# TensorE instead of SyncE as the engine that ends a log-sum-exp kernel

## The chip, the cores and the metric

The kernel runs on 1 core of one Trainium2 chip. The metric is the device time in microseconds (us). The core has five engines, each with its own instruction stream: TensorE (PE), VectorE (DVE), ScalarE (ACT), GpSimd (POOL) and SyncE (SP). An engine named with a q behind it (SPq, PEq) is that engine's sequencer, which handles waits, semaphores, branches and DMA issues itself.

## What is computed

The reference takes x of 32 x 512 x 1024 float32 and returns, for each of the 16,384 rows of 1024, the logarithm of the sum of exponentials:

```python
max_x = np.max(x, axis=-1, keepdims=True)
return (max_x.squeeze(-1) + np.log(np.sum(np.exp(x - max_x), axis=-1))).astype(np.float32)
```

## The kernel before, in words

Each of the 128 partitions holds 128 rows of 1024. The kernel does not subtract the maximum at first: it takes exp of the raw data and sums it, and a check at the end tells whether all sums are in a safe range. Only if one is not does it do the work again with the maximum taken off (the block under `nc.If`, line 258), which the inputs here do not need.

SP issues 18 loads of falling size, written out in the table `LOADS` (lines 17 to 22), into a ring of 48 rows per partition (`load`, lines 121 to 128). For each load ACT waits on a semaphore of its own (`landed`), takes exp in place (line 192), and DVE sums the rows (line 196, or line 204 for the last rows of the stream). Every engine's order is written by hand, and every wait is on a counter: `act`, `dve` and `pe` count finished instructions, and a DMA adds 16 to its semaphore when it has landed.

The end goes like this. ACT takes the logarithm of the first 112 rows (line 219), and SP stores them early (line 227, semaphore `early_store`, called `sp.sem`). PE adds up the last sums with small matmuls (lines 143, 147 and 248), so that DVE can tell with one comparison whether all is fine (`fine`, line 251). Meanwhile ACT takes the last logarithms (lines 230 and 232), and SP issues the last store (line 236, semaphore `stored`). ACT and DVE read `fine` into a register each (line 254) and branch past the second pass. Then both add 1 to `done` (lines 303 and 304).

The lines after that are those of the change. In the kernel before they all run on SP: it waits for `done` to reach 2 and for the early store (lines 305 and 306), clears all semaphores but `stored` with one instruction (line 307), and with a last instruction waits for `stored` to reach 16 and takes the 16 off again (line 309). It is the program's last instruction. POOL does nothing but set constants at the program's start. PE's last instruction is the matmul of line 147 that adds the last partial sum.

At the program's start the language puts barriers between the five engines (lines 57 and 347 in the profile): each engine adds to one semaphore with a DRAIN, POOL counts them and adds to a second one, and each engine waits for that one with an EVENT_SEMAPHORE.

Of the kernel before, what the change touches and what calls it, by code (L numbers as in the profile page):

```python
# [47 lines left out]
def kernel(  # L48
# [5 lines left out]
    nc = tc.nc  # L54
# [49 lines left out]
    landed = [nc.alloc_semaphore(f"landed{i}") for i in range(len(loads))]  # L104
# [3 lines left out]
    sp = Counted(nc, nc.sync, "early_store")  # L108
    done = nc.alloc_semaphore("done")
    again = nc.alloc_semaphore("again")  # L110
    ready = nc.alloc_semaphore("ready")
    stored = nc.alloc_semaphore("stored")
# [145 lines left out]
    with nc.If(all_fine < 1):  # L258
# [43 lines left out]

    nc.scalar.sem_inc(done, 1)
    nc.vector.sem_inc(done, 1)
    nc.sync.wait_ge(done, 2)
    nc.sync.wait_ge(sp.sem, 16)
    nc.sync.sem_clear(range(landed[0].num, stored.num))
    kind = dict(sync_type="semaphore", id=stored.num, ant_name="stored")
    nc.sync.add_instruction(mybir.InstEventSemaphore(
        name=nc.get_next_instruction_name(), engine=mybir.EngineType.SP,  # L310
        sync_info=mybir.SyncInfo(
            on_wait=[mybir.SyncWait(wait_mode="sem-ge-imm", wait_value=16, **kind)],
            on_update=[mybir.SyncUpdate(update_mode="sem-sub-imm", update_value=16, **kind)],
# [49 lines left out]
```

## Time and profile before

| | us |
|---|---|
| median of 3 runs | 162.51 (162.45 to 162.53) |
| the profiled execution, its own time | 162.54 |
| its span, first to last instruction | 161.2 |
| time outside that span | 1.34 |
| DVE busy | 120.4 |
| ACT busy | 116.2 |
| PE busy | 2.1 |

All times in the profile are counted from the first instruction, which is SP's first load. The span is that of the program's own instructions. What the time of an execution holds beyond the span, 1.34 us, has no instruction in the profile, but the trace also records updates of semaphores, and some of these come after the program's last instruction.

### The profile page before, as it was taken

Reading aid. Unit: us, or ns where it says so; the run is one execution under the profiler, and the core shown is the slowest. Engines: PE = TensorE matmul, PEld = TensorE weight load, DVE = VectorE, ACT = ScalarE, POOL = GpSimd, SP = SyncE. Lnnn points to the kernel's source line nnn. Section 1 sums busy time; section 2 is a strip of 40 time slices with the busy share of each in tenths; the row PEclk is TensorE's granted clock in tenths of the full one; section 3 lists DMA queues with packets and bytes.
Section 4 is the critical chain, followed back from the end, with each engine's and each line's share of the span. In section 5 each row is a group of like instructions: output and inputs, shape, how many; then the busy total and the mean of one; then the engine's idle time right before and its main releaser. Section 6 shows DMA issues by size and latency. Waiting matters only on the chain.

```text
span 161.2 us, 227 instructions
## 1 busy us (share of the span) xinstructions
PE 2.1 (1%) x24; PEld 1.0 (1%) x24; DVE 120.4 (75%) x57; ACT 116.2 (72%) x49; POOL 0.2 (0%) x4
## 2 busy tenths in 40 slices
PE   0000000000000000000000000000000000000022
PEld 0000000000000000000000000000000000000011
DVE  0000000009999999999999999999999995999894
ACT  3000059990799709995199949983999999989995
POOL 0000000000000000000000000000000000000000
DMA  7996996996996996996999999997999999999991
GB/s 260 520 520 276 504 520 276 504 520 276 504 520 276 504 520 276 504 520 276 463 439 439 439 423 407 445 534 331 439 439 419 434 407 430 442 419 410 410 397 25
DMA packets 2883, 67.19 MB, mean 417 GB/s; under 512 B 577, under 2 KB 705, under 8 KB 1345
## 3 DMA queue, kind: packets, MB, share of 16 engines
q1 hardware_dynamic: 2880, 67.18, 97.3%
q14 instruction: 3, 0.02, 0.0%
HBM read 67.11 MB, written 0.07 MB: 417 GB/s over the span
## 4 chain that ended last, share of the span: by engine, by line
DVE 51%; DMA 29%; ACT 16%; issue 2%; PE 0%
DVE sumexp L196 51%; DMA ring<-in_x_dram 29%; ACT ring L192 15%; ACT last_exp L170 1%; ACT res L219 0%; PE count L147 0%; DVE fine L251 0%
## 5 line engine op out<-in xcount | busy, mean ns | idle before, releaser
L196 DVE TENSOR_REDUCE sumexp<-ring 128x8 f32<-128x8192 f32 (+6 forms) x15 | 108.8, 7326 | 36.3 <-ACT ring L192 36.3
L192 ACT ACTIVATE ring<-ring 128x8192 f32<-128x8192 f32 (+15 forms) x23 | 103.8, 4571 | 41.8 <-DMA ring<-in_x_dram 41.8
L204 DVE SCALAR_TENSOR_TENSOR ring<-ring 128x512 f32<-128x512 f32 x17 | 10.7, 689 | 0.6 <-ACT ring L192 0.6
L181 ACT ACTIVATE ring<-ring 128x1024 f32<-128x1024 f32 x9 | 9.4, 1041 | 0.0
L114 ACT ACT_TABLE_LOAD x1 | 1.3, 1283 | 1.5 <-PEq L57 1.5
L143 PE MATMUL count<-far,bad 128*1 128x1 f32 x2 | 0.2, 164 | 153.7 <-DVE clamped L138 153.7
L147 PE MATMUL count<-sumexp,ones 128*1 128x1 f32 x20 | 1.8, 164 | 3.5 <-DVE ring L204 3.4
L181 ACT ACTIVATION_READ_ACCUMULATOR ring<-ring 128x1 f32 x9 | 1.7, 186 | 0.0
L204 DVE DVE_READ_ACCUMULATOR ring<-ring 128x1 f32 x17 | 1.4, 83 | 0.0
L115 DVE MEMSET ones<- 128x1 f32 x1 | 0.1, 59 | 1.5 <-PEq L57 1.5
L170 ACT ACTIVATE last_exp<-ring 128x640 f32<-128x640 f32 (+1 forms) x2 | 1.2, 591 | 0.0
L143 PEld LDWEIGHTS count<-far,bad 128*1 128x1 f32 x2 | 0.1, 80 | 153.7 <-DVE clamped L138 153.7
L147 PEld LDWEIGHTS count<-sumexp,ones 128*1 128x1 f32 x20 | 0.8, 81 | 4.4 <-DVE ring L204 4.2
L251 DVE TENSOR_SCALAR fine<-count 1x1 int32<-1x1 f32 x1 | 0.1, 147 | 0.6 <-PE count L147 0.6
L170 ACT ACTIVATION_READ_ACCUMULATOR last_exp<-ring 128x1 f32 x2 | 0.4, 186 | 0.0
L138 DVE SCALAR_TENSOR_TENSOR clamped<-clamped,sumexp 128x119 f32<-128x119 f32 x1 | 0.3, 284 | 0.0
L232 ACT ACTIVATE res<-sumexp 128x1 f32<-128x1 f32 x1 | 0.3, 294 | 0.0
L219 ACT ACTIVATE res<-sumexp 128x112 f32<-128x112 f32 x1 | 0.3, 279 | 0.0
L242 DVE SCALAR_TENSOR_TENSOR clamped<-sumexp 128x9 f32<-128x9 f32 x1 | 0.2, 169 | 0.1
L133 DVE TENSOR_SCALAR clamped<-sumexp 128x119 f32<-128x119 f32 x1 | 0.2, 222 | 0.0
L230 ACT ACTIVATE res<-sumexp 128x15 f32<-128x15 f32 x1 | 0.2, 198 | 0.0
L248 PE MATMUL count<-far,bad 128*1 128x1 f32 x2 | 0.2, 164 | 0.0
(8 smaller groups left out, 0.7 us busy)
## 6 DMA issues: line engine op xcount, KB each, us to landing
ring<-in_x_dram SPq DMA_DIRECT2D x1, 6912.0 KB, 26.0
ring<-in_x_dram SPq DMA_DIRECT2D x1, 6400.0 KB, 23.9
ring<-in_x_dram SPq DMA_DIRECT2D x1, 4608.0 KB, 17.7
ring<-in_x_dram SPq DMA_DIRECT2D x1, 3840.0 KB, 19.3
ring<-in_x_dram SPq DMA_DIRECT2D x1, 2816.0 KB, 25.6
ring<-in_x_dram SPq DMA_DIRECT2D x1, 2368.0 KB, 25.2
ring<-in_x_dram SPq DMA_DIRECT2D x1, 1696.0 KB, 21.7
ring<-in_x_dram SPq DMA_DIRECT2D x1, 1248.0 KB, 24.4
```

The lines of the kernel that those rows point to most:

```text
L114: nc.scalar.preload_act_table_set("natural_log_exp_and_others")
L133: dve.did(nc.vector.tensor_scalar(out=clamped[:, 0:LATE], in0=sumexp[:, 0:LATE], scalar1=LOW, scalar2=HIGH, op0=ALU.max, op1=ALU.min,))
L138: dve.did(nc.vector.scalar_tensor_tensor(out=clamped[:, 0:LATE], in0=clamped[:, 0:LATE], scalar=0.0, in1=sumexp[:, 0:LATE], op0=ALU.bypass ...
L143: pe.did(nc.tensor.matmul(count, lhsT=bad[:, 0:1], rhs=far, start=True, stop=False))
L147: return pe.did(nc.tensor.matmul(count, lhsT=ones, rhs=sumexp[:, c : c + 1], **kw))
L170: at = act.did(nc.scalar.activation(out=last_exp[:, here - p : end - p], in_=ring[:, here:end], func=AF.Exp, accum_out=sumexp[:, LAST : NC ...
L181: at = act.did(nc.scalar.activation(out=v, in_=v, func=AF.Exp, accum_out=sumexp[:, c : c + 1]))
L192: at = act.did(nc.scalar.activation(out=v, in_=v, func=AF.Exp))
L196: who = (dve, dve.did(nc.vector.reduce_sum(out=sumexp[:, c : c + s], in_=rows, axis=AX.X)))
L204: who = (dve, dve.did(nc.vector.scalar_tensor_tensor(out=lo, in0=lo, scalar=1.0, in1=rows[:, r, H:d], op0=ALU.mult, op1=ALU.add, accum_out ...
L219: ln_early = act.did(nc.scalar.activation(out=res[:, 0:W], in_=sumexp[:, 0:W], func=AF.Ln))
L232: ln_last = act.did(nc.scalar.activation(out=res[:, LAST:NC], in_=sumexp[:, NC : NC + 1], func=AF.Ln, bias=sumexp[:, LAST:NC]))
```

## The change

The last instructions are moved from SP to PE. SP adds 1 to `done` after it has issued the last store, as ACT and DVE do, and PE waits for 3 instead of SP for 2. The clear and the last wait are the same instructions on another engine. Nothing else differs.

```diff
     nc.scalar.sem_inc(done, 1)
     nc.vector.sem_inc(done, 1)
-    nc.sync.wait_ge(done, 2)
-    nc.sync.wait_ge(sp.sem, 16)
-    nc.sync.sem_clear(range(landed[0].num, stored.num))
+    nc.sync.sem_inc(done, 1)
+    nc.tensor.wait_ge(done, 3)
+    nc.tensor.wait_ge(sp.sem, 16)
+    nc.tensor.sem_clear(range(landed[0].num, stored.num))
     kind = dict(sync_type="semaphore", id=stored.num, ant_name="stored")
-    nc.sync.add_instruction(mybir.InstEventSemaphore(
-        name=nc.get_next_instruction_name(), engine=mybir.EngineType.SP,
+    nc.tensor.add_instruction(mybir.InstEventSemaphore(
+        name=nc.get_next_instruction_name(), engine=mybir.EngineType.PE,
         sync_info=mybir.SyncInfo(
             on_wait=[mybir.SyncWait(wait_mode="sem-ge-imm", wait_value=16, **kind)],
             on_update=[mybir.SyncUpdate(update_mode="sem-sub-imm", update_value=16, **kind)],
```

## The prediction

> **What bounds the kernel now.** I read the chain of work that ended last first, then SP's own waits, then the last instructions one by one.
>
> ```profile
> ## 4 chain that ended last, share of the span: by engine, by line
> DVE 51%; DMA 29%; ACT 16%; issue 2%; PE 0%
> ```
>
> This says that the 161.2 us go to loads, ACT and DVE. The change touches none of those instructions: by the order of instructions on each engine, DVE, ACT and POOL keep theirs, SP loses the clear and the last wait, and PE gains them behind its last matmul. So only the last two microseconds can differ. The view of DMA issues has the last store (out<-in, size, us to landing):
>
> ```profile
> out_dram<-res SPq DMA_DIRECT2D x1, 8.0 KB, 1.7
> ```
>
> It lands 1.7 us after SP issues it; it is issued at 159.45, so it lands at 161.2, which is the end of the span. The chain of work ends before it, with the comparison at line 251, because it follows no store. The end is set by the store.
>
> ```profile
> SPq L307 <- ACTq L303: 0.7, 1, 0.7
> SPq L309 <- SPq L309: 0.6, 1, 0.6
> ```
>
> These are SP's own waits. SP stood 0.7 us before the clear, until ACT's addition to `done` at line 303, and then 0.6 us before its last instruction. The second is the wait for the store. The view of single lines gives both instructions:
>
> ```profile
> L307 SPq EVENT_SEMAPHORE_RANGE_CLEAR  x1: 68/68/68, 160.5 to 160.5; - x1
> L309 SPq EVENT_SEMAPHORE  x1: 17/17/17, 161.2 to 161.2; - x1
> ```
>
> From the trace's records at full precision: ACT's addition ends at 160.493, the clear runs from 160.516 to 160.584, the store's 16 increments of `stored` come from 160.731 to 161.175 (the 15th at 160.873), and the last instruction runs from 161.191 to 161.208.
>
> **What comes behind the span.** The trace also holds updates of a semaphore that the program does not use, number 2, after and between the engines' ends:
>
> ```
> 159.522 | 160.637  160.676  160.720 | 161.352  161.396  161.434  161.468  161.515
> then resets of the semaphores 7 to 255, 161.477 to 162.085
> 162.309  162.343  162.381  162.425  162.448  162.546  162.584  162.618  162.665
> ```
>
> Nine updates, twice. I read it as a barrier of five engines, a chain up and back (five updates up, four down). The first comes at 159.522. POOL was done by 1.6, DVE and ACT only after 160.3, SP at 161.208; only PE ends just before it (its last matmul at 159.343). So PE is the first link. The second comes at 160.637, 0.144 after ACT's end. The third and fourth are POOL and DVE, idle already. The fifth comes at 161.352, 0.144 after SP's end: the same 0.144 as ACT's, so SP is the last link. Now SP comes last and the way back starts at once: 161.515 - 161.352 = 0.163 us. The second barrier starts at PE and finds all others ready: 162.665 - 162.309 = 0.356 us. That is what the first would take if PE came last.
>
> [...]
>
> **The change, part by part.**
>
> *Removed from SP, added to SP.* SP's clear (68 ns) and last wait go; SP gets one addition to `done`. Its wait of line 306 ran at 159.849, and I take the addition there: 0.63 before ACT's, so `done` is still completed by ACT at 160.493. Nothing is queued behind SP's two instructions but its link in the barrier. Cost 0.
>
> *The clear on PE.* PE has been idle since 159.343, so no program work is queued behind its new wait. The trace does not show a clear on PE. From below, SP's 68 ns; from above, three times that, 0.2 us, as the widest ratio of PE to SP for a semaphore instruction (51 to 17 ns, next view). Started by 160.55 it ends by 160.75, and the store lands at 161.175. The store's landing hides it, at either end, with 0.4 to spare; without that cover it would cost 0.07 to 0.2. Cost 0.
>
> *The last wait on PE.* The barriers at the program's start show the same kind of instruction on all engines:
>
> ```profile
> L57 SPq EVENT_SEMAPHORE  x2: 17/17/17, 1.0 to 1.4; - x2
> L57 ACTq EVENT_SEMAPHORE  x2: 17/17/17, 1.1 to 1.4; - x2
> L57 DVEq EVENT_SEMAPHORE  x2: 21/21/21, 1.1 to 1.4; - x2
> L57 PEldq EVENT_SEMAPHORE  x2: 51/51/51, 1.1 to 1.4; - x2
> ```
>
> SP needs 17 ns, PE 51. The starts, at full precision, are 1.375 for SP and 1.387 for PE after the same release: PE wakes 0.012 later. From such a wait to the engine's next instruction, in two barriers, SP needs 71 and 92 ns, ACT 92 and 91, DVE 111 and 112, PE 150 and 151. So PE's sequencer is 1.64 (151/92) to 2.11 (150/71) times as slow as SP's here, on average 1.85.
>
> *From the last wait to PE's link.* SP needs 161.352 - 161.191 = 0.161 from the start of its last instruction to its update; ACT the same. For PE the trace shows no such stretch: behind its last matmul it needs 0.179 from the matmul's end and 0.342 from its start (159.180 to 159.522). By the ratios it is 0.161 x 1.64 = 0.264 to 0.161 x 2.11 = 0.340; I take 0.161 x 1.85 = 0.298, between PE's two rows. A gain is excluded: no row has PE quicker than SP.
>
> Sum: 0.012 (later waking) + 0.298 - 0.161 = 0.137 (slower instructions) + 0.193 (the barrier goes up behind PE) = 0.342 us. With the ends of the ratio it is 0.308 and 0.384. The 0.193 contains 0.054 because DVE, having just made its own update, answers SP after 0.098 and not 0.044; without it the lower end is 0.254. What follows the first barrier (resets, second barrier) starts at PE in both kernels and moves as a whole.
>
> Against the profiled execution this is 162.54 + 0.34 = 162.88. That one lies 0.03 above the median of the runs, so the forecast is 162.51 + 0.34 = **162.85 us**; its own range is 162.76 to 162.90.
>
> **The rivals.**
>
> *PE fetches its last code late* (slower). The records show two reads of 8192 bytes of instructions near the end, at 159.830 (0.342 long) and 161.078 (0.621 long). The first starts 0.308 after PE's link. If it is PE's code for the resets, it now has time; behind a late PE it would land 0.65 to 0.93 after PE's link, while the resets (first record at 161.736, 0.221 after the barrier) would want it 0.356 + 0.221 = 0.577 after. That adds 0.07 to 0.35: 162.92 to 163.20. For it: the place in time. Against it: SP and ACT also have work there, and the records do not name the engine.
>
> *PE's sequencer is as quick as SP's here.* Then 0.137 falls away and 0.012 + 0.193 = 0.205 is left: 162.72, within the bound. For it: the 0.179 behind the matmul's end is near SP's 0.161. Against it: 51 to 17 ns. [...]
>
> *The time ends before the barrier.* The 1.34 us outside the span can lie behind it (barrier, resets and second barrier end 1.46 after it) or ahead of it. If the time closes at the last engine's own end, only 0.012 + 0.034 counts: 162.56.
>
> *Faster: the time closes on an engine other than PE.* The decisive point is again where the 1.34 lies. If the time is closed by the end of an engine's program, and PE's is not the one read, the store's landing drops out of it: the last end would be ACT's, at 160.493 instead of SP's at 161.208, 0.715 earlier: 161.80. For it: PE's share of the end is the one that the span has never had to show. Against it: all five engines are in the barrier.
>
> That the change doesn't do what it says can be left out: PE's stream has the two instructions, and nothing else is behind the store.
>
> **How the numbers follow.** About 0.2% (0.33 us) can be told from no change. Forecast 0.52, of which I give 0.34 to above 162.84 and 0.18 to below, as the point lies just above the bound; late code 0.18, slower; PE as quick as SP 0.12, same; time before the barrier 0.10, same; closed on another engine 0.08, faster. So faster 0.08, same 0.40, slower 0.52. The range leaves out the faster case and the upper part of the late code (about 0.1): 162.55 to 163.00.
>
> **What would show it.** In the changed kernel's trace the store should land as before, at 161.18; PE's last EVENT_SEMAPHORE should start at 161.20 and take 51 ns; semaphore 2 should show its first update only some 0.3 after that, all nine in one run of about 0.356, and the second run as before. The span should grow by only 0.05, and the time outside it by 0.3. If the first update comes within 0.18 of PE's last instruction, PE is as quick as SP; if the resets of 7 to 53 start later than 0.22 after the ninth update, code is late. If the store lands earlier or later by more than 0.05, the change reaches something that I hold untouched, and the forecast is wrong in its ground.

## The result, and the profile after

The changed kernel takes 162.69 us (median of 15 runs, 162.58 to 163.12) against 162.50 for the kernel before in the same comparison (median of 15 runs, 162.29 to 162.73). The ratio is 1.0016, 95% interval 1.0010 to 1.0023: slower by 0.26 us, with 0.16 to 0.37 as the interval's ends (the medians differ by 0.19, the means by 0.28). That is clear of no change, but below the 0.2% that the prediction took as its bound; the interval lies on both sides of it. A second comparison later gave 162.73 (11 runs) against 162.40 (28 runs), ratio 1.0019 (1.0010 to 1.0028).

The page of the changed kernel shows that the work itself is as it was (first the span, then the chain by engine):

```profile
span 160.9 us, 228 instructions
...
## 4 chain that ended last, share of the span: by engine, by line
DVE 52%; DMA 29%; ACT 16%; issue 2%; PE 0%
```

The span is 0.3 us *shorter* than before, while the execution's own time is 162.58, 0.04 longer than the profiled execution before. Both can only hold if the time outside the span has grown: it was 1.33 and is 1.63. The span is shorter because this execution issued its last store at 159.167 and the one before at 159.453. That is a difference between executions: in the twelve profiles of this study the issue lies between 159.167 and 159.453, in kernels with SP last (159.168, 159.181) as in kernels with another engine last. The chain in order of time shows where it comes from. Its first piece, the wait for the first load, is 0.29 us shorter (start and duration in us, before and after), and no other piece differs by more than 0.01:

```profile
0.00 22.07 DMA ring<-in_x_dram
```

```profile
0.00 21.78 DMA ring<-in_x_dram
```

So the two must be compared from the store on. The view of DMA issues gives it the same 1.7 us (1.722 before and 1.703 after, from the records):

```profile
out_dram<-res SPq DMA_DIRECT2D x1, 8.0 KB, 1.7
```

SP's own waits no longer hold the two at the end of the list before; the last store's is left as it was:

```profile
SPq L227 <- ACT res L219: 11.8, 1, 11.8
SPq L236 <- ACT res L232: 7.8, 1, 7.8
```

In the view of single lines, the clear and the last wait are now PE's (line numbers are higher by one; columns as before, duration in ns, then first and last start):

```profile
L308 PEldq EVENT_SEMAPHORE_RANGE_CLEAR  x1: 237/237/237, 160.2 to 160.2; - x1
L310 PEldq EVENT_SEMAPHORE  x1: 51/51/51, 160.9 to 160.9; - x1
```

The clear takes 237 ns instead of 68, but it ends at 160.479 and the store lands at 160.870. The last wait takes 51 ns instead of 17, as the barrier at the start had shown. Behind it, semaphore 2 gets its updates:

```
161.182 161.217 161.255 161.299 161.322 161.421 161.459 161.493 161.540
162.329 162.363 162.402 162.446 162.469 162.567 162.605 162.639 162.686
```

Before, the first update came at 159.522 and the last five of the first nine between 161.352 and 161.515. Now all nine come in one run of 0.358 us, with the same steps as the second nine. No engine had to be waited for except PE, and PE's update is the first of the nine: nothing could go ahead of it.

From the store's landing the two executions compare like this:

| us, from the step before | before (SP) | after (PE) | difference |
|---|---|---|---|
| last increment of `stored` to start of the last instruction | 0.016 | 0.028 | 0.012 |
| to that engine's update of semaphore 2 | 0.161 | 0.284 | 0.123 |
| to the ninth update | 0.163 | 0.358 | 0.195 |
| to the last of the second nine | 1.150 | 1.146 | -0.004 |
| landing to end | 1.490 | 1.816 | 0.326 |

The last row, called landing to end, is what the experiments compare: it does not contain the store's way to its landing, which differs between executions (1.70 to 2.04 us in the twelve profiles). The time of an execution follows it. In all twelve profiles the execution's own time equals the moment of semaphore 2's last update, counted from the span's start, less 0.106 to 0.125 us (162.54 and 162.665 before, 162.58 and 162.686 after).

The runs of the kernel as a whole say the same. In the second comparison each run's span is known to 0.1 us. The time outside the span is 1.34 us before (mean of 28 runs, 1.29 to 1.40) and 1.64 after (11 runs, 1.59 to 1.69), so every changed run lies above every run of the kernel before, while the spans of both scatter by 0.5 to 0.6 us.

### The profile page after: what moved, and what is told of

Its sections match the earlier page's. It is cut to its first block, busy times and chain, and to the rows that moved or that the text cites. A ratio compares the mean times of both kernels' runs of the same rounds, so it can differ in the third digit from the quotient of the medians.

```text
span 160.9 us, 228 instructions
## 1 busy us (share of the span) xinstructions
PE 2.1 (1%) x24; PEld 1.0 (1%) x24; DVE 120.3 (75%) x57; ACT 116.2 (72%) x49; POOL 0.2 (0%) x4
## 4 chain that ended last, share of the span: by engine, by line
DVE 52%; DMA 29%; ACT 16%; issue 2%; PE 0%
DVE sumexp L196 51%; DMA ring<-in_x_dram 29%; ACT ring L192 15%; ACT last_exp L170 1%; ACT res L219 0%; PE count L147 0%; DVE fine L251 0%
```

## The experiments

**The changed kernel again**, beside three others on the same chip.

> The changed kernel again, as the yardstick of the others. The stretch to be compared is the one from the store's last increment of `stored` to the last update of semaphore 2 (landing to end): 1.490 us in the profile before, 1.816 in the profile after. Theory A (the place in the barrier's chain plus PE's slower sequencer): 1.81 to 1.82 again, and a ratio of 1.0010 to 1.0025. Theory B (the profiled execution was an odd one): landing to end differs from 1.816 by more than 0.05.

Ratio 1.0019 (1.0010 to 1.0028), landing to end 1.816. Theory A holds, and the measure repeats to within 0.001 us although the store was issued 0.155 later than in the first profile.

**Other engines as the last one.** The edit is that of the change with another engine's name; those of ACT, DVE and SP that do not wait add to `done`, and the wait on `done` counts them. For ACT:

```diff
-    nc.scalar.sem_inc(done, 1)
     nc.vector.sem_inc(done, 1)
-    nc.sync.wait_ge(done, 2)
+    nc.sync.sem_inc(done, 1)
+    nc.scalar.wait_ge(done, 2)
...
```

> ACT, the second link of the chain, ends the program. Theory A: ACT's sequencer is as quick as SP's (0.161 from the last instruction to its link), but the chain now has to go up behind it, three links more; from the rows of the second barrier 162.665 - 162.343 = 0.322 instead of 0.163. Landing to end 1.49 + 0.16 = 1.65 us, time +0.16 us, ratio 1.0010. Theory C (only PE's slow sequencer counts, the place in the chain doesn't): 1.49 and ratio 1.0000. Theory D (any engine but SP costs the same fixed sum): 1.82 and ratio 1.0020.

> POOL, the third link, ends the program. Theory A: 162.665 - 162.381 = 0.284 from its link to the barrier's end instead of 0.163, so +0.12 with a sequencer like SP's: landing to end 1.61 us, up to 1.7 if POOL's last instructions are slower than SP's; no row shows them. Theory C: 1.49 if POOL is as quick as SP. Theory D: 1.82.

> DVE, the fourth link, ends the program. Theory A: 162.665 - 162.425 = 0.240 from its link to the barrier's end instead of 0.163, so +0.077; DVE wakes 0.010 later and its sequencer takes 111 to 112 ns where SP takes 71 to 92, so another 0.03 to 0.09: landing to end 1.61 to 1.67 us, +0.12 to 0.18. Theory C: only the sequencer's 0.04 to 0.10, 1.53 to 1.59. Theory D: 1.82.

| last engine | time, ratio (interval) | landing to end | last instruction to its update | its update to the ninth | expected of the latter |
|---|---|---|---|---|---|
| SP (before) | 1 | 1.490 | 0.161 | 0.163 | |
| DVE | 1.0010 (1.0001 to 1.0019) | 1.624 | 0.208 | 0.241 | 0.240 |
| ACT | 1.0015 (1.0006 to 1.0024) | 1.652 | 0.160 | 0.324 | 0.322 |
| PE (the change) | 1.0016 (1.0010 to 1.0023) | 1.816 | 0.284 | 0.358 | 0.356 |
| POOL | 1.0029 (1.0017 to 1.0041) | 2.073 | 0.579 | 0.286 | 0.284 |

The place in the chain is settled by the last two columns: the order of links is PE, ACT, POOL, DVE, SP, and an engine that comes last pays for every link behind it, to within 0.003 us in every run what the rows of the second barrier had said. DVE's 1.624 lies in the range that theory A gave for it. (PE's ratio in the table is that of the first comparison; beside the other three it is the 1.0019 above.) ACT is the cleanest case. Its last wait takes as long as SP's (columns as above),

```profile
L309 ACTq EVENT_SEMAPHORE  x1: 17/17/17, 161.4 to 161.4; - x1
```

it reaches its link in 0.160 as SP does in 0.161, and it is still 0.162 longer from landing to end. Theory C (only the sequencer's speed counts) and theory D (one sum for all engines but SP) both fall with it.

POOL's place came out as expected and its end did not: 0.579 us pass between its last instruction and its link, where theory A had put a sequencer like SP's. (Another 0.035 of its 2.073 lies between the two barriers' ends, 1.184 where all other profiles have 1.144 to 1.150; the cause is not known.) Two runs below look at that.

**Half of the change: the clear on PE, the last wait on SP.**

```diff
+    nc.sync.sem_inc(done, 1)
+    nc.tensor.wait_ge(done, 3)
+    nc.tensor.wait_ge(sp.sem, 16)
+    nc.tensor.sem_clear(range(landed[0].num, stored.num))
...
     nc.sync.add_instruction(mybir.InstEventSemaphore(
```

> Half of the change: PE clears the semaphores, SP waits for the store and is the program's last engine. Theory A: the clear on PE took 237 ns and ended 0.4 us before the store landed, so it is hidden, and SP is last in the chain as before: landing to end 1.49 us, ratio 1.0000. Rival: the clear on PE costs what it takes longer there, 0.17: 1.66 and ratio 1.0010.

Ratio 0.9996 (0.9987 to 1.0005), landing to end 1.483. The clear takes its 237 ns here too (first fence, view of single lines), and SP then stands 1.7 us for the store (second fence, SP's waits), so it costs nothing:

```profile
L308 PEldq EVENT_SEMAPHORE_RANGE_CLEAR  x1: 237/237/237, 160.2 to 160.2; - x1
```

```profile
SPq L310 <- SPq L310: 1.7, 1, 1.7
```

This run also shows that a PE which is late, but not last, costs nothing that can be measured. Its link came at 160.683, where it comes between 159.25 and 159.52 in the kernels that leave PE idle at the end, and ACT's, POOL's and DVE's followed by 160.799, long before SP's at 161.379.

**The other half: SP clears, PE waits.**

```diff
     nc.sync.sem_clear(range(landed[0].num, stored.num))
+    nc.sync.sem_inc(stored, 1)
...
+    nc.tensor.add_instruction(... EngineType.PE, wait 17 of `stored`, take 17 off)
```

> The other half: SP clears the semaphores as before and then adds 1 to `stored`, PE alone waits for the store (for 17, of which 16 are the store's) and takes 17 off. Theory A: all of the change's cost is here, landing to end 1.81 to 1.82 us, ratio 1.0020. Rival: the clear on PE is what costs, 1.49 to 1.65 here.

Ratio 1.0021 (1.0012 to 1.0030), landing to end 1.821. The whole cost is in the engine of the last wait.

**PE's sequencer by itself, and SP's.** The loop adds eight waits that are already met when the store has landed, on PE in the changed kernel and on SP in the kernel before:

```diff
+    for _ in range(8):
+        nc.tensor.add_instruction(mybir.InstEventSemaphore(... wait for 16 of `stored`, no update))
```

> The changed kernel with 8 more EVENT_SEMAPHOREs on PE ahead of the last one, each waiting for the same 16 of `stored`, so that 8 run after the store has landed. It measures PE's sequencer by itself. Theory A: PE needs 51 to 150 ns for each, so landing to end grows by 0.4 to 1.2 us over the 1.816 of the changed kernel, and by at least 1.6 times as much as SP's does in the run beside it. Rival (PE's sequencer is as quick as SP's): the same growth on both.

> The kernel before with the same 8 more EVENT_SEMAPHOREs on SP ahead of its last instruction. Theory A: SP needs 17 to 81 ns for each, landing to end grows by 0.14 to 0.65 us over the 1.490 of before. The time grows by the same amount as landing to end, for both this and the run on PE, if the time includes what comes behind the program.

The build joined the eight waits with the last instruction two by two, so that four instructions were added on each side. PE's view of single lines, then SP's:

```profile
L311 PEldq EVENT_SEMAPHORE  x4: 51/51/51, 161.1 to 161.4; - x4
```

```profile
L310 SPq EVENT_SEMAPHORE  x4: 17/28/28, 160.9 to 161.1; - x4
```

From landing to end the run on PE takes 2.269, which is 0.453 more than the changed kernel, and the run on SP 1.735, 0.245 more than the kernel before: 113 ns for each instruction on PE, 61 on SP. The ratio of the two is 1.85, which is the mean that the prediction had worked out from the start barriers. That it meets the mean so exactly is luck in part: these instructions hold two waits each, for which SP takes 28 ns where one wait took 17, while PE takes 51 for either, and the stretch from the last instruction to the link has a ratio of 1.76 (0.284 to 0.161). The rival of equal sequencers falls. The times: 1.0041 (1.0027 to 1.0055) on PE, where landing to end is longer than before by 0.779 us, 1.0048; and 1.0007 (0.9998 to 1.0016) on SP, where 0.245 us would be 1.0015, inside the interval but not shown by the times alone.

**POOL's end.** Two runs on what its 0.579 us are, the first the loop above on POOL, the second the half change with POOL in PE's place:

> With POOL last, landing to end was 2.073 us where theory A gave 1.61 to 1.7: from the start of POOL's last instruction to its link it took 0.579, not 0.161. This kernel has 8 more EVENT_SEMAPHOREs on POOL ahead of the last one, which on PE became four instructions of two waits each and 0.453 us, on SP 0.245. Theory E (POOL's sequencer is slow for everything): growth of 0.245 x 0.579/0.161, about 0.9 us. Theory F (POOL's sequencer is like SP's and a fixed piece comes between its last instruction and its link): growth of 0.2 to 0.35 us, landing to end 2.3 to 2.4.

> SP clears the semaphores and adds 1 to `stored`; POOL only waits for the store and ends the program. Theory G (the clear on POOL leaves something behind that delays its link): from POOL's last instruction to its link 0.161 to 0.25 us, landing to end about 1.65. Theories E and F: 0.58 again, landing to end 2.07.

With the extra waits landing to end is 2.384, 0.311 more than with POOL last, as theory F has it, and theory E's 0.9 falls; from the last instruction to the link it took 0.605 (the last instruction, with two waits, takes 42 ns there instead of 17). Without the clear on POOL it is still 0.578 (landing to end 2.038), so the clear leaves nothing behind and theory G falls. The times agree with both: 1.0050 (1.0034 to 1.0065) and 1.0043 (1.0027 to 1.0059). POOL's last instruction itself is no longer than SP's:

```profile
L310 POOLq EVENT_SEMAPHORE  x1: 17/17/17, 161.3 to 161.3; - x1
```

So a piece of about 0.4 us (0.579 less SP's 0.161) that grows neither with the waits nor with the clear stands between POOL's last instruction and its link. What it is has no record in the trace and stays open.

## Why the prediction was right

*What bounds the end.* Right: the last store's landing ends the program in both kernels (the last instruction starts 0.016 and 0.028 us behind it), and the work ahead of it is unchanged. One of the prediction's own tests was badly put: it asked for the store to land within 0.05 us of 161.18, and it landed at 160.87. By its own words the forecast would then have been wrong in its ground, and it was not: the issue itself moves by up to 0.29 from execution to execution. The time from the issue, 1.722 and 1.703, was the better test in these two profiles, but it too is no constant: over the twelve it runs from 1.70 to 2.04. For the same reason the span did not grow by 0.05 but shrank by 0.26; the time outside it grew by 0.30, as forecast.

*The barrier behind the program.* Right in its order and in its sum: 0.193 forecast, which is 0.356 - 0.163 from the rows of the kernel before, and 0.195 measured (0.358 - 0.163), and ACT, POOL and DVE as last ones fit it to 0.002. The pass that finds all engines ready takes 0.356 us in the trace before and 0.358 and 0.357 in the one after; its single steps there last 0.023 to 0.099.

*The clear on PE.* Its cost of 0 was right; its upper bound was not. It takes 237 ns where at most 0.2 us had been allowed. With 0.4 us of cover that made no difference, and the half change shows it: landing to end 1.483, ratio 0.9996.

*PE's waking and its way to the link.* Waking 0.012, as forecast. To the link 0.284 where 0.298 was taken (between 0.264 and 0.340): the 0.137 of the sum is 0.123. This is the only term of the sum that is off by more than 0.002; with -0.004 in the stretch behind the barrier and 0.002 more in the barrier it makes the difference between 0.342 and 0.326.

*The time.* 162.85 was forecast, with 162.55 to 163.00 as the range; the median is 162.69. The forecast difference of 0.34 lies inside the interval of the measured one (0.16 to 0.37), near its upper end. The mechanism's own size is 0.326 by the trace. The rest of the gap is most likely scatter in the span, ahead of the part that changes. The store's landing, counted from the first instruction, differs by up to 0.54 between the twelve profiles, more than the change is worth, and 15 runs do not quite average that out; the spans of the 15 runs before are not known, so this is not shown. In the second comparison, with 28 runs before, the medians differ by 0.33. Of the chances, "slower by over 0.2%" had most weight and the measured 0.16% lies just under that line; the prediction had put its point just above it and said so. Its bound of 0.2% for what can be told from no change was too wide: the interval here reaches 0.07% to either side.

*The rivals.* Late code falls: the reads of 8192 bytes of instructions start 0.346 and 1.642 us after the issue of the store in the changed kernel, 0.377 and 1.625 before, so they do not follow PE's end, and the resets of semaphores 7 to 53 start 0.219 after the barrier, as before (0.221). PE as quick as SP falls by the extra waits: an instruction of this kind costs PE 113 ns and SP 61. Why PE needs more is open. A time that ends before the barrier falls too, and with it the faster case: in twelve profiles the time keeps a nearly fixed distance (0.106 to 0.125 us) from the second barrier's last update, with any of the five engines last.

## What to carry to other kernels

The last thing in this program is a wait, and the engine that waits matters although it computes nothing: in all twelve profiles the five engines pass a barrier in a fixed order after the program, and the time includes it. That order is PE, ACT, POOL, DVE, SP, and landing to end was 1.490 us with SP last and 1.624 to 2.073 with another engine in its place. So where a trace shows such a barrier, the engine at its end (SP here) should be the one that waits for the last store, and instructions behind that wait should be few (113 ns each on PE, 61 on SP, with two waits in each). An engine that finishes late but not last cost nothing here (the clear on PE and the last wait on SP: ratio 0.9996), so clears and the like can go where the store's landing covers them, as it covered the 237 ns of the clear on PE. On this kernel the choice is worth about 0.2% of the time.

## What was not expected of the hardware

The last of the store's 16 increments comes 0.27 to 0.62 us after the 15th in all twelve profiles. In the three in which the first late read of 8192 bytes of instructions starts 0.63 to 0.64 us after the store's issue, the store lands 2.01 to 2.04 us after its issue; in the other nine the read starts after 0.35 to 0.38 and the store lands after 1.70 to 1.87. That is a correlation; whether the read holds the store up was not tried. It is as large as the whole effect of the change.

The clear of the same 25 semaphores takes 68 ns on SP, 146 on ACT, 178 on POOL, 199 on DVE and 237 on PE.

On POOL, 0.58 to 0.61 us pass from the last instruction to its link in the barrier, in three kernels, while its semaphore instruction with a single wait takes 17 ns, as SP's does.
